# Sums of weight blocks in a two-layer hybrid trunk: two of four formed by accumulating transfers

## The chip, the cores and the metric

The kernel runs on one core of a Trainium2 chip. A core has TensorE for matrix products (PE in the profile, with its weight loader PEld), VectorE (DVE), ScalarE (ACT), GpSimd (POOL) and SyncE (SP), each with an instruction queue of its own that it works off in order, and sixteen DMA engines that all queues share. Waits between queues are on semaphores. The metric is the device time of one execution in microseconds; three runs of the kernel before gave 1565.7 to 1568.12, median 1567.72.

## The reference

Two layers act on 256 tokens of width 1024, all in float32. Each is a half-step SwiGLU feed-forward (FFN), a mixer, and a second FFN; a norm closes the trunk:

```python
for l in range(DEPTH):                       # DEPTH = 2
    h = h + 0.5 * swiglu(rms_norm(h, ffn1_norm[l]), ffn1_w_in[l], ffn1_w_out[l])
    u = rms_norm(h, mix_norm[l])
    ...
    h = h + merged @ w_out[l]
    h = h + 0.5 * swiglu(rms_norm(h, ffn2_norm[l]), ffn2_w_in[l], ffn2_w_out[l])
return rms_norm(h, final_norm)
```

`swiglu(x, w_in, w_out)` is `(silu(gate) * up) @ w_out`, with `gate` and `up` the halves of `x @ w_in` and 2816 inner channels. The mixer (a Mamba-2 branch beside a gated DeltaNet branch) is not touched by the change. There are four FFNs in all.

## The kernel before

**Forms.** All weights stand in one array `wst`, laid out in the order of use, in blocks of 128 x 1024 floats (512 KB). A block is loaded by SP into a raw slot (`wraw`, five slots, `NRAW`), then split for TensorE into a high half on ScalarE (`whi`, line 163) and a rest on VectorE (`wlo`, line 170). The profile names the lines of the helpers: 67 for `act` on ScalarE, 70 for `tt` and 73 for `stt` on VectorE. Such a pair is a form; there are five form slots (`NSPL`). Every product is three matmuls: high by high, low by high, high by low. A raw slot is free again when its block has been split, a form slot when the last product with it is done. `plan_ffn` writes the sequence of loads (`stream`) and of forms (`plan`) ahead of time; `take` gives the next form and keeps loads and splits running ahead by as many as the slots allow. The order of instructions on each engine's queue is set when the kernel is built, by a scheduler that goes by the order of writing and by when it reckons slots to be free; so a load into a slot that is free early can stand far ahead of its use.

**One FFN** follows the string `FFN`, `f` + 8 `c` + `A` + 4 `c` + `A` + 4 `c` + `A` + 2 `c` + `A` + 2 `c` + `BdBBBddddd`. `f` is a first chunk of 256 channels by tokens (four forms); each `c` is a chunk of 128 gate and 128 up channels (two forms, tile `fc`). The product with `w_out` is in part done by Winograd's form of Strassen's method, which needs seven products of 2 x 2 blocks in place of eight. Its weight blocks are b11, b12, b22 and b21, for two pairs of row blocks at a time, so a group has seven forms `q0` to `q6`, four in `A` (tiles `p`) and three in `B` (tiles `o`). Four groups cover sixteen row blocks; six blocks are multiplied directly (`d`). The closing stage is `BdBBBddddd`; in its last five `d` all five forms are needed within the first 15 matmuls, since the first half of the tokens goes through all five `d` before the second.

**Sums of blocks, before.** `A` loads b11 into a slot of its own (`wfirst`, tags `y0` to `y3`, four slots that the mixer uses too), and b12 and b22 into raw slots. Between its four splits VectorE does three subtractions in place (function `less`): `wfirst<-wraw,wfirst` twice and `wraw<-wraw` once. `B` loads b22 and b21 anew, subtracts once more, `wfirst<-wraw,wfirst`, and splits three forms. That is four subtractions a group, 64 in the kernel. The input's block sums, formed on VectorE by `block_sums` from a chunk's result `g2` (tiles `sf`), carry the matching signs. `join` adds the products of a pair's banks to `h` (eight VectorE instructions in two parts, on `h`, `u2`, `u4`, `u5`).

**GpSimd** does little here: it fills tiles with zeros in the mixer and computes powers (`rsqrt`, line 190), among them `zz`, the one that each norm waits for between `zz` on VectorE (line 78) and `hn`. The norm that follows an FFN runs while TensorE is at the second half of the last five `d`.

Of the kernel before, what the change touches and what calls it, by code (L numbers as in the profile page):

```python
# [52 lines left out]
def trunk_kernel(ctx, tc, x, wst, wsm, norms, lpar, rpar, cst, out):  # L53
# [32 lines left out]
    def trb(name):  # L86
        return trp.tile([P, 512], F32, tag="tr", name=name)
# [12 lines left out]
    def plan_plain(j, n):  # L100
        for i in range(j, j + n):
            stream.append(i)
            plan.append(("d", [len(stream) - 1], len(stream)))
        return j + n

    def plan_ffn(j):


        o, j2, held = j + 4 * FC, j + 4 * FC + 22, []
        for kind in FFN:  # L110
            if kind in "fc":
                j = plan_plain(j, 4 if kind == "f" else 2)
            elif kind == "d":
                o = plan_plain(o, 1)
            else:
                if kind == "A":
                    where = [len(stream) + i for i in range(3)]
                    stream.extend(range(o, o + 3))
                    held.append((where, o + 2))
                    o += 4  # L120
                    for i, need in enumerate((2, 3, 3, 3)):
                        plan.append((f"q{i}", where, where[0] + need))
                else:
                    where, b22 = held.pop(0)
                    where += [len(stream) + 1, len(stream)]
                    stream.extend([b22, b22 + 1])
                    for i in range(4, 7):
                        plan.append((f"q{i}", where, len(stream)))
        return j2
# [5 lines left out]
    n_raw = len(stream)  # L135
    first = {js[0] for kind, js, _ in plan if kind == "q0"}
    n_forms = len(plan)
    state = {"loaded": 0, "prepped": 0, "taken": 0, "last": None, "hold": False, "behind": {}, "first": 0}
    raws, halves = {}, {}

    def load(j):
# [5 lines left out]
        state["last"] = nc.sync.dma_start(r[:], wst[stream[j] // 2, :, (stream[j] % 2) * 1024 :][:, 0:1024])  # L147
        raws[j] = r

    def prep(i):  # L150
        kind, js, _ = plan[i]
        hi = wpool.tile([P, 1024], F32R, tag="whi", name="whi", bufs=NSPL)
        lo = wpool.tile([P, 1024], F32R, tag="wlo", name="wlo", bufs=NSPL)

        def less(o, a, b):
            tt(raws[js[o]][:], raws[js[a]][:], raws[js[b]][:], ALU.subtract)


        r = raws[js[{"q2": 1, "q4": 4, "q5": 3}.get(kind, 0)]]
        with ExitStack() as behind:  # L160
            for ins in state["behind"].pop(i, ()):
                behind.enter_context(tc.issue_after(ins))
            act(hi[:], r[:])
            if kind == "q1":
                less(1, 2, 1)
            elif kind == "q2":
                less(0, 2, 0)
            elif kind == "q4":
                less(0, 3, 0)
            tt(lo[:], r[:], f(hi[:]), ALU.subtract)  # L170
            if kind == "q0":
                less(0, 1, 0)
        for o in {"d": (0,), "q2": (1,), "q3": (2,), "q4": (4,), "q5": (3,), "q6": (0,)}.get(kind, ()):
            raws.pop(js[o])
        halves[i] = (hi, lo)
# [6 lines left out]
    def take():  # L182
        j = state["taken"]
        state["taken"] = j + 1
        ahead("loaded", min(plan[min(j + NSPL, n_forms) - 1][2] + NRAW - 1, n_raw), load)
        ahead("prepped", min(j + 1 if state["hold"] else j + NSPL, n_forms), prep)
        return halves.pop(j)
# [205 lines left out]
    def join(pb):  # L393
# [10 lines left out]
        stt(u5[:], pb[5][:], 0.5, u2[:], ALU.mult, ALU.add)  # L404
        tt(hv[1][0], hv[1][0], u2[:], ALU.add)
        tt(hv[1][1], hv[1][1], u5[:], ALU.add)
        yield
# [26 lines left out]
    def ffn(nxt):  # L434
# [19 lines left out]
        def block_sums(p, g2):  # L454
# [35 lines left out]
        for c in range(FC - 1):  # L490
# [18 lines left out]
            if todo[0] == "A":  # L509
                if not pb:  # L510
                    pb.update({i: trb(f"p{i}") for i in (1, 6, 5, 7)})
                four = [
                    (pb[1], lambda p: stat(2 * p, 0), PAIRS[n]),
                    (pb[5], lambda p: sums(p, 0), PAIRS[n]),
                    (pb[7], lambda p: sums(p, 2), PAIRS[n]),
# [849 lines left out]
```

## Time and profile before

| | |
|---|---|
| median of three runs | 1567.72 us |
| the profiled execution | 1568.61 us, span 1566.8 us |
| TensorE busy, granted clock | 98% of the span, 0.999 |
| VectorE busy | 80% |
| ScalarE busy | 61% |
| GpSimd busy | 3%, 60 instructions |
| transfers | 293.14 MB, 187 GB/s in the mean |

The profiled execution's own time is 1.8 us above its span and 0.9 us above the median. The busy shares are means over stages: TensorE's 98% says that little of the time is lost, and the view of waits says where. In a row of the order of time stand start, duration, engine, line, operation, result and operands, and in brackets the engine's idle time before it and what ended that. The loader (PEld) runs ahead of the products, so an idle time there is not lost in full.

### The profile page before, as it was taken

How to read it: one execution, taken by the hardware profiler on the slowest of the kernel's cores; microseconds unless marked ns; L12 is line 12 of the kernel's file. 1: busy time of each engine (PE TensorE's matmuls, PEld its weight loads, DVE VectorE, ACT ScalarE, POOL GpSimd, SP SyncE). 2: the span in 40 equal slices, each digit the busy share in tenths (PEclk: the TensorE clock that was granted, in tenths of full speed). 3: DMA queues.
4: the chain of work that ended last, by engine and by line, in shares of the span. 5: the costliest groups of instructions: out<-in, count | busy, mean ns of one | idle time of the engine just before them, and what ended most of it. 6: DMA issues, size and time to landing. Idle time of an engine off the chain costs nothing.

```text
span 1566.8 us, 28951 instructions
## 1 busy us (share of the span) xinstructions
PE 1535.5 (98%) x11452; PEld 1382.9 (88%) x11452; DVE 1252.7 (80%) x1888; ACT 949.7 (61%) x1534; POOL 53.7 (3%) x60
## 2 busy tenths in 40 slices
PE   8999999999999999999999999999999999999997
PEld 7999779999988888999799997899898888889995
DVE  6878869967899766878878887799589997677886
ACT  5656567766665545656555565676756665455554
POOL 0000010000000000000000002010000000000000
PEclk9999999999999999999999999999999999999999
DMA  8665565653565656565665557566445556556554
GB/s 294 215 203 178 197 215 175 179 160 113 177 215 162 193 198 196 170 212 188 229 215 189 174 186 223 182 190 188 116 136 202 175 178 209 192 179 192 170 185 134
DMA packets 94222, 293.14 MB, mean 187 GB/s; under 512 B 22325, under 2 KB 23301, under 8 KB 93062
## 3 DMA queue, kind: packets, MB, share of 16 engines
q1 hardware_dynamic: 94086, 291.29, 57.5%
q8 instruction: 90, 1.47, 0.4%
q14 instruction: 46, 0.38, 0.1%
HBM read 289.33 MB, written 1.92 MB: 186 GB/s over the span
## 4 chain that ended last, share of the span: by engine, by line
PE 67%; DVE 16%; DMA 6%; issue 5%; ACT 4%; POOL 1%; SPq 1%; POOLq 0%; ACTq 0%; DVEq 0%
PE fc L301 7%; PE fc L307 7%; DVE wlo L70 7%; PE fc L306 7%; DMA wraw<-in_wst_dram 5%; PE t L297 3%; PE t L296 3%; PE t L298 3%; PE b L298 3%; PE b L297 2%; PE b L296 2%; ACT whi L67 2%; DVE ca L73 1%; PE xs L301 1%; PE xs L306 1%
## 5 line engine op out<-in xcount | busy, mean ns | idle before, releaser
L70 DVE TENSOR_TENSOR wlo<-wraw,whi 128x1024 fp32r<-128x1024 f32 x488 | 591.3, 1220 | 173.2 <-ACT whi L67 165.2
L67 ACT ACTIVATE whi<-wraw 128x1024 fp32r<-128x1024 f32 x488 | 511.5, 1059 | 275.7 <-PE fc L306 85.5
L307 PE MATMUL fc<-uW,wlo 128*128 128x256 f32 x1280 | 354.7, 277 | 0.0
L301 PE MATMUL fc<-uW,whi 128*128 128x256 f32 x1280 | 354.0, 277 | 0.0
L306 PE MATMUL fc<-uW,whi 128*128 128x256 f32 x1260 | 348.1, 276 | 0.0
L301 PEld LDWEIGHTS fc<-uW,whi 128*128 128x128 f32 x1280 | 240.4, 188 | 0.8
L307 PEld LDWEIGHTS fc<-uW,wlo 128*128 128x128 f32 x1280 | 240.4, 188 | 0.0
L306 PEld LDWEIGHTS fc<-uW,whi 128*128 128x128 f32 x1260 | 236.5, 188 | 0.8
L67 ACT ACTIVATE whi<-wfirst 128x1024 fp32r<-128x1024 f32 x64 | 68.0, 1062 | 59.2 <-PE fc L306 34.0
L296 PE MATMUL t<-whi,uW 128*128 128x512 f32 x256 | 102.1, 400 | 0.0
L297 PE MATMUL t<-wlo,uW 128*128 128x512 f32 x256 | 100.8, 394 | 0.5 <-DVE wlo L70 0.5
L298 PE MATMUL t<-whi,uW 128*128 128x512 f32 x256 | 100.7, 394 | 0.0
L70 DVE TENSOR_TENSOR wlo<-wfirst,whi 128x1024 fp32r<-128x1024 f32 x64 | 78.0, 1218 | 6.8 <-ACT whi L67 5.9
L296 PE MATMUL b<-whi,bh 128*128 128x512 f32 x192 | 76.3, 399 | 0.0
L297 PE MATMUL o<-wlo,gh 128*128 128x512 f32 x160 | 65.4, 409 | 9.8 <-DVE wlo L70 9.6
L297 PE MATMUL b<-wlo,bh 128*128 128x512 f32 x192 | 74.9, 390 | 0.0
L298 PE MATMUL b<-whi,bl 128*128 128x512 f32 x192 | 74.3, 394 | 0.6 <-DVE bl L70 0.6
L70 DVE TENSOR_TENSOR wfirst<-wraw,wfirst 128x1024 f32<-128x1024 f32 x48 | 58.5, 1220 | 20.2 <-DMA wraw<-in_wst_dram 19.9
L301 PE MATMUL xs<-uW,whi 128*128 128x256 f32 x256 | 73.0, 285 | 0.0
L307 PE MATMUL xs<-uW,wlo 128*128 128x256 f32 x256 | 71.5, 279 | 0.0
L306 PE MATMUL xs<-uW,whi 128*128 128x256 f32 x256 | 71.3, 279 | 0.0
L298 PE MATMUL o<-whi,gl 128*128 128x512 f32 x160 | 62.6, 391 | 0.0
(319 smaller groups left out, 3401.3 us busy)
## 6 DMA issues: line engine op xcount, KB each, us to landing
wraw<-in_wst_dram SPq DMA_DIRECT2D x504, 512.0 KB, 4.7
wfirst<-in_wst_dram SPq DMA_DIRECT2D x16, 512.0 KB, 5.4
dc<-rdram SPq DMA_DIRECT2D x8, 1024.0 KB, 8.4
nw<-in_norms_dram SPq DMA_DIRECT2D x6, 512.0 KB, 6.1
gb<-rdram SPq DMA_DIRECT2D x8, 256.0 KB, 5.5
h<-in_x_dram SPq DMA_DIRECT2D x4, 256.0 KB, 5.5
out_dram<-fo SPq DMA_DIRECT2D x4, 256.0 KB, 2.0
dq<-X SPq DMA_DIRECT2D x2, 256.0 KB, 5.7
```

The costliest lines, as they stand in the source:

```text
L67: return A.activation(out=o, in_=i, func=func, **kw)
L70: return V.tensor_tensor(out=o, in0=a, in1=b, op=op)
L73: return V.scalar_tensor_tensor(out=o, in0=a, scalar=s, in1=b, op0=op0, op1=op1)
L296: PE.matmul(ps, lh, rh, start=start, stop=False)
L297: PE.matmul(ps, lh, rl, start=False, stop=False)
L298: return PE.matmul(ps, ll, rh, start=False, stop=stop)
L301: PE.matmul(ps, wh, mh, start=start, stop=False)
L306: PE.matmul(ps, wh, ml, start=False, stop=False)
L307: PE.matmul(ps, wl, mh, start=False, stop=stop)
```

## The change

A group now has one sum tile, `wsum`, in the slots that were `wfirst`'s. SP loads b11 into it, and GpSimd issues a transfer of b12 that adds to what is there (`accum_op`), so b11 + b12 is there without VectorE. `A` loads b12, b22 and, a second time, b11 into raw slots. VectorE adds b22 to the raw b12 and to `wsum`; after the last split of `A` (`q3`) GpSimd issues a second accumulating transfer, of b21, and the sum of all four blocks stands ready for `q6`. `B` loads b22 and b21 into raw slots, which are split as they are (`q4`, `q5`). So VectorE does two additions a group in place of four subtractions, SP loads six blocks a group in place of five (one into the sum tile), and GpSimd issues two accumulating transfers a group, 32 in all. Signs that the sums lose are moved to `block_sums` and `join`; the first two products of `A` change places. The loads ahead are now bounded by counting raw slots alone (`limit`).

```diff
     def plan_ffn(j):
...
+        for at, kind in enumerate(FFN):
+            if at in spots:
+                y = len(stream)
+                stream.extend([("y", o1 + 4 * q), ("+", o1 + 4 * q + 1, y)])
+                begun.append(y)
+                q += 1
...
+            elif kind == "A":
+                y, u = begun.pop(0), len(stream)
+                stream.extend([("w", o + 1), ("w", o + 2), ("w", o)])
+                plan.append(("q1", (y, u, u + 1), u + 2))
+                plan.append(("q0", (u + 2, y, u + 1), u + 3))
+                plan.append(("q2", (u,), u + 3))
+                plan.append(("q3", (y, o + 3), u + 3))
+                held.append((y, o + 2))
+                o += 4
...
+                y, b22 = held.pop(0)
+                stream.append(("w", b22))
+                plan.append(("q4", (len(stream) - 1,), len(stream)))
+                stream.append(("w", b22 + 1))
+                plan.append(("q5", (len(stream) - 1,), len(stream)))
+                plan.append(("q6", (y,), len(stream)))
...
+    def add_to(r, i):
+        G.dma_start(out=r[:], in_=tile_of(i), accum_op=ALU.add)
+
     def load(j):
-        if j in first:
-            r = slots.tile([P, 1024], F32, tag=f"y{state['first']}", name="wfirst")
+        kind, i = stream[j][:2]
+        if kind == "+":
+            add_to(raws[stream[j][2]], i)
+            return
+        if kind == "y":
+            r = slots.tile([P, 1024], F32, tag=f"y{state['first']}", name="wsum")
...
             act(hi[:], r[:])
-            if kind == "q1":
-                less(1, 2, 1)
-            elif kind == "q2":
-                less(0, 2, 0)
-            elif kind == "q4":
-                less(0, 3, 0)
+            if kind in ("q0", "q1"):
+                to, by = (raws[k][:] for k in js[1:])
+                tt(to, to, by, ALU.add)
             tt(lo[:], r[:], f(hi[:]), ALU.subtract)
-            if kind == "q0":
-                less(0, 1, 0)
...
+        if kind == "q3":
+            add_to(r, js[1])
...
-        stt(u4[:], pb[5][:], 0.5, u2[:], ALU.mult, ALU.add)
-        tt(hv[0][1], hv[0][1], u4[:], ALU.add)
+        stt(u4[:], pb[5][:], -0.5, u2[:], ALU.mult, ALU.add)
+        tt(hv[0][1], hv[0][1], u4[:], ALU.subtract)
...
-            tt(s1, a21, a22, ALU.add)
+            tt(s1, a21, a22, ALU.subtract)
             tt(s3, a11, a21, ALU.subtract)
             tt(s2_, s1, a11, ALU.subtract)
-            tt(s4, a12, s2_, ALU.subtract)
+            tt(s4, a12, s2_, ALU.add)
```

VectorE's queue in the first FFN, from the splits of the last chunk's blocks to the first forms of the second `B`. Before (`wfirst_567` and `wfirst_900` are the b11 slots of the first two groups, `wraw_1703` and `wraw_1741` their b21):

```order
L70 TENSOR_TENSOR wlo_1730<-wraw_1569,whi_1729 128x1024 [waits DMAHW7_49,Activation_49]
L70 TENSOR_TENSOR wfirst_567<-wraw_1703,wfirst_567 128x1024 [waits DMAHW1_49]
L70 TENSOR_TENSOR wlo_1746<-wraw_1691,whi_1745 128x1024 [waits DMAHW0_49,Activation_49]
L70 TENSOR_TENSOR wfirst_900<-wraw_1741,wfirst_900 128x1024 [waits DMAHW4_49]
L70 TENSOR_TENSOR wlo_1751<-wraw_1703,whi_1750 128x1024 [waits PE_49,Activation_49]
L70 TENSOR_TENSOR wlo_1808<-wfirst_567,whi_1807 128x1024 [waits PE_49,Activation_49]
L70 TENSOR_TENSOR g2_1739<-sg_1803,fc_1740 128x256 [waits Activation_49]
L73 SCALAR_TENSOR_TENSOR h_78<-p1_846,h_78 128x512 [waits Activation_49]
L73 SCALAR_TENSOR_TENSOR u2_1966<-p6_847,half_1965 128x512
L73 SCALAR_TENSOR_TENSOR u4_1967<-p5_848,u2_1966 128x512 [waits DVE_49]
L70 TENSOR_TENSOR wfirst_1230<-wraw_1811,wfirst_1230 128x1024 [waits DMAHW6_49]
L70 TENSOR_TENSOR wlo_1814<-wraw_1715,whi_1813 128x1024 [waits DMAHW2_49,PE_49,Activation_49]
```

The same place now (`wraw_1703` and `wraw_1715` are b22 and b21 of the first group, `wsum_358` its sum tile, `wraw_1727` the single `d`):

```order
L70 TENSOR_TENSOR wlo_1742<-wraw_1581,whi_1741 128x1024 [waits DMAHW3_49,Activation_49]
L70 TENSOR_TENSOR wlo_1756<-wraw_1703,whi_1755 128x1024 [waits DMAHW4_49,Activation_49]
L70 TENSOR_TENSOR wlo_1762<-wraw_1715,whi_1761 128x1024 [waits DMAHW5_49,PE_49,Activation_49]
L70 TENSOR_TENSOR wlo_1819<-wsum_358,whi_1818 128x1024 [waits DMASW4_49,PE_49,Activation_49]
L70 TENSOR_TENSOR g2_1751<-sg_1814,fc_1752 128x256 [waits Activation_49]
L73 SCALAR_TENSOR_TENSOR h_78<-p1_854,h_78 128x512 [waits Activation_49]
L73 SCALAR_TENSOR_TENSOR u2_1972<-p6_853,half_1971 128x512
L73 SCALAR_TENSOR_TENSOR u4_1973<-p5_852,u2_1972 128x512 [waits DVE_49]
L70 TENSOR_TENSOR h_78<-h_78,u4_1973 128x512 [waits DVE_49]
L70 TENSOR_TENSOR wlo_1825<-wraw_1727,whi_1824 128x1024 [waits DMAHW6_49,PE_49,Activation_49]
L73 SCALAR_TENSOR_TENSOR u2_1972<-p7_855,u2_1972 128x512
L70 TENSOR_TENSOR g2_1751<-sg_1876,fc_1817 128x256 [waits Activation_49]
```

The three subtractions are gone, two more joins stand ahead of the last chunk's `g2`, and the split of the sum tile waits on a semaphore of the accumulating transfers (DMASW).

GpSimd's queue between the mixer of the first layer and the third FFN, before (`zz_6769` and `zz_6805` are the powers of the norm into the second FFN, one for each half of the tokens, the last two those of the norm into the third):

```order
L190 TENSOR_TENSOR srr_6215<-sss_6207,mhalf_96 128x2 [waits DVE_49]
L190 TENSOR_TENSOR zz_6769<-zz_6769,mhalf_96 128x1 [waits DVE_49]
L190 TENSOR_TENSOR zz_6805<-zz_6805,mhalf_96 128x1 [waits DVE_49]
L190 TENSOR_TENSOR zz_8776<-zz_8776,mhalf_96 128x1 [waits DVE_49,Pool_49]
L190 TENSOR_TENSOR zz_8812<-zz_8812,mhalf_96 128x1 [waits DVE_49,Pool_49]
```

And now, from the second FFN's norm to the third's (`wsum_7015` to `wsum_7963` are the second FFN's sum tiles, `wsum_9030` to `wsum_9978` the third's):

```order
L212 TENSOR_TENSOR zz_6813<-zz_6813,mhalf_96 128x1 [waits DVE_49]
L165 DMA wsum_7015<-in_wst_dram 128x1024 [waits DVE_49]
L165 DMA wsum_7378<-in_wst_dram 128x1024 [waits DVE_49]
L165 DMA wsum_7715<-in_wst_dram 128x1024 [waits DVE_49]
L165 DMA wsum_7963<-in_wst_dram 128x1024 [waits DVE_49]
L165 DMA wsum_9030<-in_wst_dram 128x1024 [waits DMASW4_49,DMAHW5_49,DMASW0_49,DVE_49]
L165 DMA wsum_9393<-in_wst_dram 128x1024 [waits DMASW5_49,DMAHW1_49,DMASW1_49,DVE_49]
L165 DMA wsum_9730<-in_wst_dram 128x1024 [waits DMASW6_49,DMAHW4_49,DMASW2_49,DVE_49]
L165 DMA wsum_9978<-in_wst_dram 128x1024 [waits DMASW7_49,DMAHW4_49,DMASW3_49,DVE_49]
L212 TENSOR_TENSOR zz_8792<-zz_8792,mhalf_96 128x1 [waits DVE_49,Pool_49]
```

An FFN's four first accumulations stand together ahead of its four second ones (the second FFN's are the first four rows of transfers here), and the third FFN's first ones stand ahead of its own norm's powers.

SP's queue at the end of the second FFN, before (`wfirst_9886` and `wfirst_10166` are b11 slots of the third FFN):

```order
L147 DMA wfirst_9886<-in_wst_dram 128x1024 [waits DVE_49]
L147 DMA wraw_8601<-in_wst_dram 128x1024 [waits DMAHW6_49,DMAHW5_49,DVE_49]
L147 DMA wraw_8643<-in_wst_dram 128x1024 [waits DMAHW7_49,DVE_49]
L147 DMA wfirst_10166<-in_wst_dram 128x1024 [waits DVE_49]
L147 DMA wraw_8655<-in_wst_dram 128x1024 [waits DMAHW0_49,DVE_49]
```

Now (`wraw_8637` and `wraw_8659` are the last two `d`, the next four the third FFN's `f`, `wraw_8713` its first channel block):

```order
L177 DMA wsum_9730<-in_wst_dram 128x1024 [waits DMASW6_49,DVE_49]
L177 DMA wraw_8637<-in_wst_dram 128x1024 [waits DMAHW6_49,DMAHW5_49,DVE_49]
L177 DMA wraw_8659<-in_wst_dram 128x1024 [waits DMAHW7_49,DVE_49]
L177 DMA wraw_8671<-in_wst_dram 128x1024 [waits DMAHW0_49,DVE_49]
L177 DMA wraw_8683<-in_wst_dram 128x1024 [waits DMAHW2_49,DVE_49]
L177 DMA wraw_8695<-in_wst_dram 128x1024 [waits DMAHW3_49,DMAHW1_49,DVE_49]
L177 DMA wraw_8711<-in_wst_dram 128x1024 [waits DMAHW5_49,DVE_49]
L177 DMA wraw_8713<-in_wst_dram 128x1024 [waits DMAHW6_49,DVE_49]
L177 DMA wsum_9978<-in_wst_dram 128x1024 [waits DMAHW4_49,DMASW7_49]
```

The load for the third FFN's fourth sum tile has moved behind the last `d`, the four `f` and a channel block.

More of the change, by code (lines that the diff above doesn't have):

```diff
@@ L106, in plan_ffn @@
     def plan_ffn(j):
-        o, j2, held = j + 4 * FC, j + 4 * FC + 22, []
-        for kind in FFN:
+        o, j2, begun, held = j + 4 * FC, j + 4 * FC + 22, [], []
+        spots, q = [], 0
+        for at, kind in enumerate(FFN):
+            if kind == "A":
+                spots.append(at - 2)
+        o1 = o + FFN[: FFN.index("A")].count("d")
+        for at, kind in enumerate(FFN):
+            if at in spots:
[3 more added lines that the diff above has]
+                q += 1
             if kind in "fc":
@@ L135, in trunk_kernel @@
     n_raw = len(stream)
-    first = {js[0] for kind, js, _ in plan if kind == "q0"}
+    limit = []
+    for _, _, need in plan:
+        m, room = need, NRAW
+        while m < n_raw:
+            room -= stream[m][0] == "w"
+            if not room:
+                break
+            m += 1
+        limit.append(m)
     n_forms = len(plan)
@@ L184, in take @@
         state["taken"] = j + 1
-        ahead("loaded", min(plan[min(j + NSPL, n_forms) - 1][2] + NRAW - 1, n_raw), load)
+        ahead("loaded", limit[min(j + NSPL, n_forms) - 1], load)
         ahead("prepped", min(j + 1 if state["hold"] else j + NSPL, n_forms), prep)
@@ L510, in ffn @@
                 if not pb:
[L511 removed]
+                    pb.update({i: trb(f"p{i}") for i in (5, 6, 1, 7)})
                 four = [
+                    (pb[5], lambda p: sums(p, 0), PAIRS[n]),
                     (pb[1], lambda p: stat(2 * p, 0), PAIRS[n]),
[L514 removed]
                     (pb[7], lambda p: sums(p, 2), PAIRS[n]),
```

31 lines of the change are left out of this document (9 added, 22 removed).

## The prediction

> **What bounds the kernel now.** I read the busy times first, then who waits for whom on TensorE, then the order of time around the waits, then the transfers.
>
> ```profile
> PE 1535.5 (98%) x11452; PEld 1382.9 (88%) x11452; DVE 1252.7 (80%) x1888; ACT 949.7 (61%) x1534; POOL 53.7 (3%) x60
> ...
> PE o L297 <- DVE wlo L70: 9.6, 16, 1.4
> PE hnT L262 <- DVE hn L73: 5.1, 6, 0.9
> ...
> PEld o L297 <- DVE wlo L70: 21.6, 32, 1.8
> PEld hnT L262 <- DVE hn L73: 6.3, 4, 2.4
> ```
>
> TensorE is the bound: 98%. What another engine can give back is TensorE's waiting, and the last lines say where most of that is: 32 weight loads of the output products (`o`) waited 21.6 us for VectorE's low half `wlo` (total, times, longest). These are eight in each of the four closing stages of an FFN (the string `BdBBBddddd`); the stages with the products `p` have no such row. In order of time, in the first FFN (start, duration, then in brackets the idle time and its releaser):
>
> ```profile
> 140.34 0.39 PE L296 MATMUL p<-whi,gh 128*128 128x512 f32 x1
> 145.80 0.28 PE L301 MATMUL fc<-uW,whi 128*128 128x256 f32 x1
> 156.83 0.39 PE L296 MATMUL o<-whi,bsc 128*128 128x512 f32 x1
> 169.19 0.39 PE L296 MATMUL o<-whi,gh 128*128 128x512 f32 x1
> 170.05 0.39 PE L298 MATMUL o<-whi,gl 128*128 128x512 f32 x1
> 193.74 0.39 PE L296 MATMUL t<-whi,uW 128*128 128x512 f32 x1
> ...
> 169.71 0.19 PEld L297 LDWEIGHTS o<-wlo,gh 128*128 128x128 f32 x1 [0.56 <-DVE wlo L70]
> 179.45 0.19 PEld L297 LDWEIGHTS o<-wlo,gh 128*128 128x128 f32 x1 [1.21 <-DVE wlo L70]
> ```
>
> A group `A` is 24 matmuls from 140.34 to 145.80: 0.2275 us each. Two such steps should take 0.455; from 169.19 to 170.05 they took 0.86, so the 0.56 of idle loader cost 0.405, 0.16 less than it reads (the loader has slack). Over all: 21.6 - 32 x 0.16 = 16.5 us. This is the most that the change can win, if it touches nothing else.
>
> Why VectorE is late there:
>
> ```profile
> 147.32 1.22 DVE L70 TENSOR_TENSOR wfirst<-wraw,wfirst 128x1024 f32<-128x1024 f32 x1
> 148.45 1.22 DVE L70 TENSOR_TENSOR wlo<-wraw,whi 128x1024 fp32r<-128x1024 f32 x1
> 152.87 1.23 DVE L70 TENSOR_TENSOR wfirst<-wraw,wfirst 128x1024 f32<-128x1024 f32 x1 [3.19 <-DMA wraw<-in_wst_dram]
> 154.01 1.22 DVE L70 TENSOR_TENSOR wlo<-wraw,whi 128x1024 fp32r<-128x1024 f32 x1
> ...
> 158.70 1.23 DVE L70 TENSOR_TENSOR wfirst<-wraw,wfirst 128x1024 f32<-128x1024 f32 x1
> 167.30 1.23 DVE L70 TENSOR_TENSOR wfirst<-wraw,wfirst 128x1024 f32<-128x1024 f32 x1 [0.77 <-DMA wraw<-in_wst_dram]
> 178.19 2.34 DVE L70 TENSOR_TENSOR wlo<-wraw,whi 128x1024 fp32r<-128x1024 f32 x2
> 180.46 1.28 DVE L70 TENSOR_TENSOR h<-h,u 128x512 f32<-128x512 f32 x2
> 181.66 1.21 DVE L70 TENSOR_TENSOR wlo<-wraw,whi 128x1024 fp32r<-128x1024 f32 x1
> ...
> L70 DVE TENSOR_TENSOR g<-sg,fc 128x256 f32<-128x256 f32 x80 | 33.0, 413 | 0.0
> L70 DVE TENSOR_TENSOR gl<-g,gh 128x512 fp32r<-128x512 f32 x40 | 27.3, 683 | 0.0
> ```
>
> Four subtractions of the closing stage stand between the splits, and twice VectorE, whose queue is in order, idled at one whose block had not landed while splits of older blocks stood behind it (3.19 us at 152.87). Issue to issue a split costs 1.14 us (two from 178.19 to 180.46).
>
> Set T = 156.83, the first closing product. TensorE needs 18 x 0.2275 = 4.1 us for a `B`, 2.7 for the single `d`; the last five `d` start at T + 19.1 and take a new form every 3 x 0.2275 = 0.68, the fifth's low half at T + 22.05. Before, three of the eighteen forms were ready at T (five slots, two still with the last chunk). So VectorE owed 15 x 1.14 = 17.1, two subtractions 2.3, the eight joins of `h` and `u` 5.1 (two in 1.28 at 180.46), two `g` and a `gl` 1.5, and idled 0.77: 26.8 us for 22.05. It came 4.7 late; by the waits of this FFN and of the second, each in a window of its own, TensorE's loader stood 4.4 there:
>
> ```profile
> PEld o L297 <- DVE wlo L70: 4.4, 8, 1.2
> ...
> PEld o L297 <- DVE wlo L70: 6.6, 8, 1.8
> ```
>
> **The change, part by part.**
>
> ```profile
> L70 DVE TENSOR_TENSOR wfirst<-wraw,wfirst 128x1024 f32<-128x1024 f32 x48 | 58.5, 1220 | 20.2 <-DMA wraw<-in_wst_dram 19.9
> L70 DVE TENSOR_TENSOR wraw<-wraw 128x1024 f32<-128x1024 f32 x16 | 19.5, 1218 | 0.1
> L67 ACT ACTIVATE whi<-wfirst 128x1024 fp32r<-128x1024 f32 x64 | 68.0, 1062 | 59.2 <-PE fc L306 34.0
> ```
>
> *Subtractions removed.* 48 + 16 become 2 x 16 additions: 32 x 1.22 = 39 us off VectorE, 9.8 an FFN, two in each `A` and one in each `B`. In the `A` stages this buys nothing: TensorE does not wait there. In the closing stage all four go, and with them the queueing behind unlanded blocks. The order now has the joins ahead of T, save one `u5` and two `h`. Four forms are ready at T, so VectorE owes 14 x 1.14 + 1.1 (one `g`, one `gl`) + 1.9 (three joins) = 19.0 us for 22.05. The limit is then the five form slots: the fifth `d` gets its slot when the last `B` product ends, T + 19.1; 1.06 us on ScalarE (the `whi` row), 1.22 on VectorE and about 0.2 between give T + 21.6, 0.45 early. So the 16.5 us go, if the blocks land in time.
>
> *Loads added.* An FFN's plain loads grow from 70 to 74, and eight accumulating transfers come on top.
>
> ```profile
> q1 hardware_dynamic: 94086, 291.29, 57.5%
> ...
> wraw<-in_wst_dram SPq DMA_DIRECT2D x504, 512.0 KB, 4.7
> dc<-rdram SPq DMA_DIRECT2D x8, 1024.0 KB, 8.4
> ...
> 10.00:20.00 10.00, 9.22 (x35) 6.88 (x36) 8.82 (x12) 7.79 (x14) 0.56 (x1) 1.00 1.03 404
> ...
> 770.00:775.00 5.00, 3.83 (x14) 2.21 (x13) 4.87 (x6) 2.12 (x2) 0.00 (x0) 1.00 1.03 388
> ```
>
> 291.29 MB took 57.5% of 1566.8 us: 524,288 bytes cost 1.62 us of all sixteen engines, 1.30 at the best rate seen (404 GB/s). No accumulating transfer is in this trace. Its price P lies between a plain one's 1.3 and, since it fetches the block from HBM and the sum from SBUF, two plain ones' 3.24; I take 3.24, nearest to the row of the 1024 KB transfer, which lands in 8.4 us where 512 KB takes 4.7. Per FFN that is 74 x 1.62 + 8 x 3.24 = 146 us of the 183 between the first `f` (10.8) and 193.74: it fits. The tightest stretch is from the third `A` to the fourth, 5.46 + 11.03 = 16.5 us: seven plain loads and one accumulation, 11.3 + 3.2 = 14.6. With five raw slots and nine blocks in 19.1 us a block may take 10.6 us from issue to split; less the 2.3 of its two passes and some queueing, landing may take about 7.5. So no stall in three FFNs; I leave 0.5 us in each. The second FFN's closing stage also carries the third's four sums: nine blocks, three `y` loads and three accumulations in 22 us: 19.4 + 9.7 at the mean rate, 15.6 + 9.7 at the best. That is more than 22 and the limit that 770 to 775 already touched (share 1.03), but the sums are not due until the next FFN's first `A`, and blocks are up to five ahead; I take 2 us there, between 0 and the 6.6 - 8 x 0.16 = 5.3 that its waits cost now.
>
> The Trainium skill, "Collectives: The Full Stack", section "The bandwidth ceiling: the fold count and why AG ≠ RS ≠ AR", says that an adding transfer runs at half the rate of a copy, not for the addition but because it has two source reads. By it P would be 3.24, by the plain row 1.62, and the sum 1.5 us smaller; no run here shows it yet.
>
> *What joins GpSimd's queue.* 32 transfers. Ahead of the power of the norm between FFN 2 and 3 now stand the third FFN's four first accumulations, the last waiting for a `y` load that SP has behind the load for the first channel chunk, whose slot the fifth `d` frees.
>
> ```profile
> 780.56 0.55 POOL L190 TENSOR_TENSOR zz<-zz,mhalf 128x1 f32<-128x1 f32 x1 [174.24 <-DVE zz L78]
> ...
> DMA to landing us min/median/max: 3.4/5.4/7.9
> ```
>
> By the numbers above that load goes out at T + 21.7 and lands at T + 25.1 to 29.6 (the `wfirst` range); the power is due at about T + 28, 1.9 after the last product of the first half. Delay 0 to 1.6 us and the issue itself (0.2 to 2.2, GpSimd's own instructions); I take 1. The other norms' accumulations are issued long before. The number of forms, hence of splits on ScalarE and VectorE, stays; the signs and the order of two products change no count. Both cost nothing with no cover needed.
>
> Sum: 16.5 - 1.5 - 2 - 1 = 12 us off the profiled 1568.6, that is 1556.6; the median of the runs is 0.9 below the profiled one, so 1556.
>
> **Rivals.**
>
> *The accumulating transfers starve the raw blocks: slower.* Place: `A` to `A` and the closing stages. For it: at 5.1 us the 16.5-us stretch is full (11.3 + 5.1), and a block that lands 1 us later costs a fifth of that for each of some 14 blocks. Against it: traffic averages 57.5%, and P would have to be three plain transfers. From 5.1 it decides. At 7 the stretch overruns by 1.8 in each FFN and the closing stages keep their waits: 1568.6 + 7 = 1576; at 10 an FFN needs 120 + 80 = 200 us for 183, +68. I price it at 1580. Chance 0.25.
>
> *The waits change their name only.* The closing stage waits for landing blocks instead of subtractions: for it, the 3.19 us at 152.87 are a transfer's; against it, that block was the ninth ahead and held back splits whose data were there. Half to four fifths of the wait stays: 1562 to 1567. Chance 0.13.
>
> *GpSimd's queue.* The delayed power alone costs at most 3.8 us, once; it only widens the other two. If accumulations are issued late as well because GpSimd's issue crawls beside VectorE, it ends near 1572. Chance 0.04. Against it: fills of 1.81 us on GpSimd left a split beside them at 1.22:
>
> ```profile
> 973.72 1.81 POOL L660 MEMSET AT<- 128x2048 f32 x1
> ...
> 973.39 1.22 DVE L70 TENSOR_TENSOR wlo<-wraw,whi 128x1024 fp32r<-128x1024 f32 x1
> ```
>
> **Numbers.** Forecast 0.58 (own range 1549 to 1560: all 16.5 us and the lowest run's 2.9 below the profiled one at one end, only 8 us won at the other). The second rival is half a gain over 0.2% (3.1 us, about what a measurement of this kernel can tell from no change), half within it. Faster 0.58 + 0.06 = 0.64, same 0.07, slower 0.25 + 0.04 = 0.29. The range to 1582 takes in the slower cases up to P of about 7.
>
> **What would show it.** Right: the wait of `o` L297 for `wlo` falls from 21.6 to below 7, no new wait in `p` or `fc`; the VectorE groups of 48 and 16 become two of 16; a second queue of 16.8 MB appears and plain loads land in 5 to 6 us. Wrong: `fc` or `p` waits for whi or wlo with a transfer behind it, landing beyond 7.5 us, or GpSimd's `zz` starts some us after VectorE's.

## The result, and the profile after

The changed kernel takes 1559.73 us (median of six runs, 1556.05 to 1564.55), the kernel before beside it 1567.05 (six runs, 1565.7 to 1568.85): a ratio of 0.9951, 95% interval 0.9939 to 0.9963, so 7.3 us or 0.49% faster. The profiled execution took 1558.56 us with a span of 1556.8, which is 10.0 less than the span before. The forecast was 12 us less, 1556.

From the page of the changed kernel, the busy times, the transfer queues (packets, MB, share of the engines) and the landing times from issue:

```profile
PE 1530.0 (98%) x11452; PEld 1384.0 (89%) x11452; DVE 1216.8 (78%) x1856; ACT 946.5 (61%) x1534; POOL 82.6 (5%) x92
...
q1 hardware_dynamic: 96390, 299.68, 57.5%
q0 software_dynamic: 4608, 16.78, 6.2%
...
wraw<-in_wst_dram SPq DMA_DIRECT2D x520, 512.0 KB, 4.9
wsum<-in_wst_dram POOLq DMA_DIRECT2D x32, 512.0 KB, 8.0
wsum<-in_wst_dram SPq DMA_DIRECT2D x16, 512.0 KB, 6.4
```

From its view of waits, those of the loader (total, times, longest):

```profile
PEld hnT L284 <- DVE hn L73: 8.1, 5, 2.7
PEld o L319 <- DVE wlo L70: 3.9, 4, 1.1
...
PEld o L318 <- ACT whi L67: 2.6, 3, 2.2
```

And VectorE's groups of additions (busy, mean ns, idle time ahead):

```profile
L70 DVE TENSOR_TENSOR wraw<-wraw 128x1024 f32<-128x1024 f32 x16 | 19.6, 1225 | 37.1 <-DMA wraw<-in_wst_dram 37.1
L70 DVE TENSOR_TENSOR wsum<-wsum,wraw 128x1024 f32<-128x1024 f32 x16 | 19.5, 1219 | 0.1
```

The wait for the low half fell from 21.6 us in 32 waits to 3.9 in 4, the groups of 48 and 16 subtractions are two of 16 additions, and a second queue of 16.78 MB is there. New is a wait for `whi` of 2.6 us, and the wait for the norm (`hnT`) grew by 1.8. No row of `p` or `fc` is among the waits. VectorE waits 37.1 us for blocks at the first addition of `A`, but TensorE does not feel it.

Where the time went shows best in the four closing stages, each from its first product `o` to the first product of what follows (the fourth, which has nothing behind it, to its own last product). In windows cut at these starts (length, then busy time and count of TensorE, its loader, VectorE, ScalarE and GpSimd; granted clock, transfers' share, GB/s), first the kernel before:

```profile
156.80:193.70 36.90, 35.37 (x154) 27.27 (x153) 31.84 (x37) 22.04 (x26) 0.55 (x1) 1.00 0.58 194
747.10:786.20 39.10, 35.55 (x154) 27.25 (x153) 33.01 (x39) 22.03 (x26) 0.55 (x1) 1.00 0.69 237
931.00:968.00 37.00, 35.56 (x155) 27.31 (x154) 32.09 (x38) 22.05 (x26) 0.55 (x1) 1.00 0.60 196
1522.10:1559.80 37.70, 34.44 (x146) 26.20 (x144) 30.51 (x37) 18.44 (x23) 0.55 (x1) 1.00 0.43 139
```

And the changed kernel:

```profile
156.60:190.10 33.50, 33.50 (x155) 27.82 (x153) 27.76 (x32) 22.18 (x26) 0.56 (x1) 1.00 0.61 202
743.10:784.30 41.20, 36.02 (x154) 28.64 (x153) 26.94 (x30) 21.96 (x26) 4.03 (x5) 0.96 0.83 255
928.80:963.50 34.70, 33.94 (x154) 27.81 (x153) 28.43 (x33) 22.06 (x26) 0.56 (x1) 1.00 0.58 198
1516.60:1549.60 33.00, 32.76 (x145) 26.81 (x145) 26.08 (x30) 18.57 (x23) 0.56 (x1) 1.00 0.44 144
```

By the exact starts three stages are 2.2 to 4.7 us shorter, and the second is 2.1 longer. In sum that is 8.2 us; the other 1.8 of the profiled gain are small shifts elsewhere, 1.4 of it in the two mixers. The second stage is the one with GpSimd's four transfers in it (4.03 us of GpSimd, 5 instructions) and with a granted clock of 0.96.

What happens there in the changed kernel, in the order of time (start, duration, then in brackets the idle time and its releaser):

```profile
766.74 1.06 ACT L67 ACTIVATE whi<-wraw 128x1024 fp32r<-128x1024 f32 x1 [2.68 <-DMA wraw<-in_wst_dram]
767.85 0.50 PE L318 MATMUL o<-whi,gh 128*128 128x512 f32 x1 [1.74 <-ACT whi L67]
769.70 0.63 PE L320 MATMUL o<-whi,gl 128*128 128x512 f32 x1
770.12 0.63 PE L318 MATMUL o<-whi,gh 128*128 128x512 f32 x1
...
776.15 0.21 DVE L78 TENSOR_SCALAR zz<-ss 128x1 f32<-128x1 f32 x1 [0.79 <-ACT junk L67]
778.34 0.86 POOL L165 DMA_DIRECT2D wsum<-in_wst_dram  x1 [15.27 <-DMA wsum<-in_wst_dram]
778.90 0.88 POOL L212 TENSOR_TENSOR zz<-zz,mhalf 128x1 f32<-128x1 f32 x1
780.62 0.66 PE L284 MATMUL hnT<-cs,hn 128*128 128x128 f32 x4 [1.92 <-DVE hn L73]
```

Two windows there, with the columns of the windows above:

```profile
765.40:768.80 3.40, 1.21 (x3) 0.45 (x3) 0.98 (x1) 1.06 (x1) 0.00 (x0) 0.99 1.06 298
769.00:772.50 3.50, 3.40 (x9) 2.73 (x10) 0.74 (x2) 0.72 (x2) 0.00 (x0) 0.55 1.02 359
```

And its transfers from 743 to 775 us, the queue of the accumulations and the median landing times:

```profile
q0 software_dynamic: 432, 1.57, 25.7%
...
wraw<-in_wst_dram SPq DMA_DIRECT2D x12, 512.0 KB, 7.6
wsum<-in_wst_dram POOLq DMA_DIRECT2D x3, 512.0 KB, 9.2
```

Three things add up. The blocks land in 7.6 us here, for a median of 4.9 over the whole kernel, while the transfers' share is at 1.02 to 1.06: ScalarE waits 2.68 us for one, and TensorE behind it. Then the clock is granted at half speed for about 3.4 us: a matmul every 0.42 in place of 0.2275, some 1.7 us lost. And GpSimd issues the third FFN's fourth accumulation, whose tile's first load landed only then, ahead of the norm's power: VectorE's `zz` is done at 776.36, the power starts at 778.90, and TensorE stands 1.92.

### The profile page after: what moved, and what is told of

The parts are those of the page before. It is cut to its first block, busy times and chain, and to the rows that moved or that the text cites. A ratio compares the mean times of both kernels' runs of the same rounds, so it can differ in the third digit from the quotient of the medians.

```text
span 1556.8 us, 28984 instructions
## 1 busy us (share of the span) xinstructions
PE 1530.0 (98%) x11452; PEld 1384.0 (89%) x11452; DVE 1216.8 (78%) x1856; ACT 946.5 (61%) x1534; POOL 82.6 (5%) x92
## 3 DMA queue, kind: packets, MB, share of 16 engines
q1 hardware_dynamic: 96390, 299.68, 57.5%
q0 software_dynamic: 4608, 16.78, 6.2%
HBM read 314.50 MB, written 1.92 MB: 203 GB/s over the span
## 4 chain that ended last, share of the span: by engine, by line
PE 78%; DVE 10%; DMA 5%; ACT 3%; issue 3%; POOL 1%; SPq 0%; POOLq 0%; ACTq 0%; DVEq 0%
PE fc L329 9%; PE fc L323 9%; PE fc L328 9%; DVE wlo L70 5%; PE t L319 3%; PE t L320 3%; PE t L318 3%; PE b L320 3%; DMA wraw<-in_wst_dram 3%; PE b L319 3%; PE b L318 2%; PE o L320 2%; PE p L319 2%; PE o L319 2%; PE p L320 2%
## 5 line engine op out<-in xcount | busy, mean ns | idle before, releaser
L70 DVE TENSOR_TENSOR wlo<-wraw,whi 128x1024 fp32r<-128x1024 f32 x504 | 610.7, 1220 | 167.6 <-ACT whi L67 161.1
L67 ACT ACTIVATE whi<-wraw 128x1024 fp32r<-128x1024 f32 x504 | 527.5, 1058 | 273.9 <-PE fc L328 83.9
L67 ACT ACTIVATE whi<-wsum 128x1024 fp32r<-128x1024 f32 x48 | 50.8, 1059 | 30.1 <-PE fc L328 25.2
L70 DVE TENSOR_TENSOR wlo<-wsum,whi 128x1024 fp32r<-128x1024 f32 x48 | 58.6, 1220 | 12.8 <-ACT whi L67 12.7
L318 PE MATMUL o<-whi,gh 128*128 128x512 f32 x160 | 63.2, 395 | 1.7 <-ACT whi L67 1.7
```

Source lines behind the costliest of these rows:

```text
L67: return A.activation(out=o, in_=i, func=func, **kw)
L70: return V.tensor_tensor(out=o, in0=a, in1=b, op=op)
L318: PE.matmul(ps, lh, rh, start=start, stop=False)
```

## The experiments

The runs lay on several chips, on which the kernel before took 1567.1 to 1570.4 us, so each is compared with the kernel before on its own chip. The lengths of the four closing stages, in us, are from each kernel's profiled execution.

| kernel | ratio to before, 95% interval | FFN 1 | FFN 2 | FFN 3 | FFN 4 |
|---|---|---|---|---|---|
| before | 1 | 36.9 | 39.1 | 36.9 | 37.7 |
| changed | 0.9951 (0.9939 to 0.9963) | 33.6 | 41.2 | 34.7 | 33.0 |
| changed, again | 0.9952 (0.9939 to 0.9964) | 35.9 | 41.9 | 34.3 | 33.2 |
| no_closing_less | 0.9897 (0.9880 to 0.9915) | 33.6 | 33.6 | 33.6 | 32.4 |
| no_less | 0.9895 (0.9878 to 0.9913) | 33.7 | 33.8 | 33.6 | 32.4 |
| no_plus | 0.9890 (0.9874 to 0.9905) | 33.6 | 33.6 | 33.6 | 33.0 |
| fourth_behind | 0.9955 (0.9943 to 0.9968) | 37.0 | 39.1 | 36.6 | 32.4 |
| plus_behind | 0.9926 (0.9913 to 0.9938) | 36.8 | 34.2 | 34.4 | 33.1 |
| sums_in_order | 1.0019 (1.0009 to 1.0029) | 35.8 | 36.2 | 36.8 | 33.8 |
| plus_twice | 1.0117 (1.0098 to 1.0136) | 36.6 | 51.4 | 36.0 | 35.6 |
| pool_less | 0.9974 (0.9962 to 0.9985) | 36.1 | 36.6 | 36.0 | 36.8 |
| six_raw | 0.9917 (0.9905 to 0.9929) | 33.6 | 33.6 | 33.6 | 32.4 |
| late_add | 0.9935 (0.9920 to 0.9950) | 34.5 | 35.5 | 34.2 | 36.8 |
| six_raw_late_add | 0.9878 (0.9860 to 0.9896) | 33.6 | 33.5 | 33.6 | 32.4 |

The theory: the closing subtractions on VectorE are the loss and the change removes it; what it loses again is the transfers' crowding and GpSimd's queue at the end of the second FFN. The rivals: VectorE's load weighs everywhere; the accumulations cost everywhere; or they cost nothing and the plain loads do.

### What VectorE's subtractions cost

**no_closing_less**

```diff
-            elif kind == "q4":
-                less(0, 3, 0)
```

> The kernel before, with the one subtraction in each B left out (16 of 64; the products of these blocks are then wrong), nothing else changed. The closing stages of the kernel before are 16.9 us longer in sum than those of the kernel without accumulations. If VectorE's debt in the closing stages is the loss, four subtractions of 1.14 us less there, and no block to wait for in them, leave a debt of some 1 to 2 us a stage at most: 10 to 15 us less than the kernel before. If the blocks' landing sets it (the rival of waits that change their name), 5 us or less.

Measured: 1552.06 us for 1568.46, 16.4 less. All four stages have the length of TensorE's work alone, called bare from here on: 33.6 us, and 32.4 for the fourth. The window of the second:

```profile
744.10:777.70 33.60, 33.60 (x154) 27.90 (x154) 27.58 (x31) 22.07 (x26) 0.55 (x1) 1.00 0.77 254
```

TensorE is busy all of the window, and no wait of `o` for `wlo` is left among the waits. The gain is above the 10 to 15 expected: no debt of 1 to 2 us a stage stayed.

**no_less**

```diff
         def less(o, a, b):
-            tt(raws[js[o]][:], raws[js[a]][:], raws[js[b]][:], ALU.subtract)
+            pass
```

> The kernel before, with all 64 subtractions left out (its products are wrong), the loads as they were. First theory: the closing stages fall to 33.6 us each and nothing else moves, 16 to 18 us less than the kernel before and within 3 us of the kernel without the subtraction in B, since in the stages A TensorE does not wait for VectorE. Second: VectorE's 80% weighs on every stage, then the other 48 subtractions bring as much again and the chunks and groups A get shorter too, over 20 us less.

Measured: 1551.94, 16.5 less. The 48 subtractions of `A`, 58 us of VectorE, are worth 0.1 us, which is nothing that can be told apart. So the 16 in `B` are the whole loss, and the rival that VectorE weighs everywhere falls.

### What the accumulations cost

**again**: the changed kernel once more, unaltered.

> The changed kernel once more, for its spread and for a second profile. If the slow clock in the second FFN's closing stage (0.50 for 3.4 us from 768.85) is a regular part of the change, the same stage shows it again and the median lies at 1558 to 1561. If it is chance, the stage may go without it, and the profiled run is then some 1.6 us shorter for that alone.

Measured: 1561.9 for 1569.64. The second stage is as long again, 41.9 us, with 3.10 us of TensorE's wait for the norm; the slow clock came behind that wait and lay over the stage's last products. That some slow stretch comes is not chance: the mean granted clock is 0.996 to 0.998 in each of the eleven executions of the changed kernel, and 0.999 in eleven of the fifteen of the kernel before on this chip. What moves from one execution to the next is the first FFN's closing stage: 35.9 us here for 33.6, from the same instructions.

**no_plus**

```diff
     def add_to(r, i):
-        G.dma_start(out=r[:], in_=tile_of(i), accum_op=ALU.add)
+        pass
```

> All 32 accumulating transfers are left out (so the sums are not formed); everything else stays. First theory: what the accumulations cost lies in the second FFN's closing stage alone (4.5 us of loader waits there, 1.6 of slow clock, 2.1 for the norm's power behind the fourth accumulation): 5 to 7 us less, 1553 to 1555 by median, and the other three FFNs keep their lengths within 0.5 us. Second theory: the accumulations slow the blocks everywhere: all four FFNs get shorter, 1549 or less. Third: the accumulations are hidden and the plain loads do it: within 2 us of the changed kernel, the waits for whi stay at 768 and 769.

Measured: 1552.34, that is 17.3 less than before and 9.6 less than the changed kernel beside it. The closing stages are the bare 33.6 us, and the clock does not fall. The cost is more than the first theory's 5 to 7 us. Between the two profiled executions (spans of 1562.3 and 1550.3) 8.3 us lie in the second FFN's closing stage, but 2.3 in the first's and 0.9 in the others. By the starts of their products, chunks and groups `A` are the same to 0.1 us with and without accumulations. So the accumulations cost in closing stages alone, and 74 plain loads an FFN in place of 70 cost nothing that can be seen. How they reach the first of these stages is open: none is issued in it, and the last one ahead of it (at 144.80 in "again") is 12.7 us earlier. What can be seen is a late block: ScalarE waited 4.12 us for one until 153.61 there, 3.8 ahead of the stage, and in the first profile 3.83 until 150.67, 5.9 ahead.

### Queue or transfers

**fourth_behind**

```diff
-            add_to(raws[stream[j][2]], i)
+            with ExitStack() as behind:
+                if state["first"] == 0:
+                    behind.enter_context(tc.issue_after(state["pow"].ins))
+                add_to(raws[stream[j][2]], i)
```

> Only the fourth of the first accumulations of an FFN is queued on GpSimd behind the power of that FFN's norm; the other three, and all plain loads, stay where they are. If the queue and the transfers are two costs that add, this takes back the 2.1 us of the power alone: 1.5 to 2.5 us less than the changed kernel, and the second FFN's closing stage keeps its loader waits of some 4.5 us and the slow clock. If the wait for the power was hidden behind the late blocks, or the fourth accumulation also slows the blocks, 0 or over 4.

Measured: 1561.79 for 1568.46, the changed kernel's ratio. In its profiled execution TensorE waits no more for the norm at that place; in the order of time VectorE's part and GpSimd's power start 0.36 us apart:

```profile
783.46 0.21 DVE L78 TENSOR_SCALAR zz<-ss 128x1 f32<-128x1 f32 x1 [0.79 <-ACT junk L67]
...
783.82 0.56 POOL L215 TENSOR_TENSOR zz<-zz,mhalf 128x1 f32<-128x1 f32 x1 [13.41 <-DVE zz L78]
```

The second stage is 39.1 us, 2.1 shorter than the changed kernel's, and keeps its late blocks and slow clock, as expected. But stages 1 and 3 were longer in this execution, which was among the slowest of its twelve (1557.77 to 1566.86); the median shows no gain. The queue's 2 us are seen in place, and not in the whole.

**plus_behind**

```diff
-            add_to(raws[stream[j][2]], i)
+            with tc.issue_after(state["pow"].ins):
+                add_to(raws[stream[j][2]], i)
```

> Only the four first accumulations of an FFN are queued on GpSimd behind the power of that FFN's norm; the loads of the tiles stay where they are. First theory: the power starts 0.4 us after VectorE's part again (2.1 us back) and the second FFN's closing stage has three accumulations less, some 9 us of all sixteen engines, so the waits of 4.5 us and the slow clock go too: 1553 to 1556. If the three plain loads of the sums are enough to fill the stage, only the 2.1 come back: 1557 to 1558.

Measured: 1557.48, 4.4 less than the changed kernel beside it. The second closing stage falls from 41.9 to 34.2 us, although the plain loads of the sums are still issued in it (at 754.3, 758.9 and 770.7 us). So it was the accumulations that filled it, and with them the slow clock is gone from the stage. The range of its runs is 3 us for 5 (five runs each); the first stage is 36.8 in the profiled one.

**sums_in_order**

```diff
+SPOTS = [4, 8, 12, 16]
...
-        spots, q = [], 0
-        for at, kind in enumerate(FFN):
-            if kind == "A":
-                spots.append(at - 2)
+        spots, q = SPOTS, 0
...
+                behind.enter_context(tc.issue_after(state["last"].ins))
```

> The plain load of each sum is queued on SP behind the block load that stands before it in the stream, at chunks 4, 8, 12 and 16 of its own FFN, so neither these loads nor the accumulations can run in the closing stage of the FFN before. First theory: 1552 to 1555, the second FFN's closing stage is as short as the first's (waits under 1 us, no slow clock, no wait for the norm at the third FFN's start), the rest unchanged. Rival: the transfers only move, and chunks or groups A of the same FFN now wait (fc or p waits for whi): 1558 or more.

Measured: 1572.62, slower than before; the rival holds. In its view of waits are such of `fc` and `p` that the changed kernel has not:

```profile
PEld o L319 <- DVE wlo L71: 11.6, 21, 1.1
...
PEld p L319 <- DVE wlo L71: 3.9, 7, 1.0
PEld fc L329 <- DVE wlo L71: 3.7, 5, 1.1
```

By the starts of its stages, four chunks took up to 23.5 us for 21.9 and an `A` up to 6.4 for 5.46, some 8 us in FFN 2 to 4. In the changed kernel the scheduler has put the first loads of FFN 2 and 4, and so their first accumulations, into the mixers (from 526.7 and 1300.3 us), where nothing waits for them. Where they run decides what they cost.

### How far from the threshold

**plus_twice**

```diff
-        G.dma_start(out=r[:], in_=tile_of(i), accum_op=ALU.add)
+        for _ in range(2):
+            G.dma_start(out=r[:], in_=tile_of(i), accum_op=ALU.add)
```

> Every accumulating transfer is issued twice (the sums are then wrong), so one sum takes 6.0 us of all sixteen engines for 3.0 and the kernel moves 33.6 MB on this queue. By the prediction's threshold (5.1 us) the stretch from the third A to the fourth overruns by about 1 us in each FFN and the closing stages keep waits: slower than the kernel before, 1572 or more by median. Rival: the accumulations hurt only where they stand in the second FFN's closing stage and in GpSimd's queue: 5 to 8 us over the changed kernel, all of it at the end of the second FFN.

From its page, the queue of the accumulations, and a window of the second closing stage:

```profile
q0 software_dynamic: 9216, 33.56, 11.7%
...
780.00:785.00 5.00, 2.81 (x4) 1.08 (x4) 2.37 (x2) 2.00 (x2) 1.75 (x2) 0.50 1.03 357
```

Measured: 1587.56, 19.1 more than before. At 2.9 us each (11.7% of the 1586.5 us span over 64 transfers), a sum step takes 5.8 us of all engines, above the 5.1 at which the prediction had it decide, and slower it is. The place is mostly another: 17.8 us over 33.6 lie in the second closing stage, where TensorE did four matmuls in 5 us at half clock (the clock was at half for 13.7 us of this stage, which can cost 6.8 at most); the three others are 2.4 to 3.2 over, and chunks and groups of the first FFN 4.3.

### A better version

The first runs say that 16 subtractions are the loss, so they could go to GpSimd, with no transfer added.

**pool_less**

```diff
             elif kind == "q4":
-                less(0, 3, 0)
+                G.tensor_tensor(out=raws[js[0]][:], in0=raws[js[3]][:], in1=raws[js[0]][:], op=ALU.subtract)
```

> The kernel before with its 16 closing subtractions on GpSimd in place of VectorE, no accumulating transfer, the 48 others left on VectorE. [...] If a subtraction takes GpSimd over some 5 us, or slows VectorE's splits beside it, the last form of a B waits for it: 0.995 to 1.01.

Measured: 1564.78 for 1569.37, 4.6 less where 16 were to be had. GpSimd's group of them:

```profile
L169 POOL TENSOR_TENSOR wfirst<-wraw,wfirst 128x1024 f32<-128x1024 f32 x16 | 44.1, 2758 | 563.3 <-DMA wraw<-in_wst_dram 419.5 <-DVE wlo L70 143.8
```

And in the order of time, GpSimd and VectorE in the first FFN's closing stage:

```profile
156.93 3.05 POOL L169 TENSOR_TENSOR wfirst<-wraw,wfirst 128x1024 f32<-128x1024 f32 x1 [1.07 <-DMA wraw<-in_wst_dram]
...
158.56 2.51 DVE L70 TENSOR_TENSOR wlo<-wraw,whi 128x1024 fp32r<-128x1024 f32 x1
...
164.74 2.62 POOL L169 TENSOR_TENSOR wfirst<-wraw,wfirst 128x1024 f32<-128x1024 f32 x1 [4.75 <-DMA wraw<-in_wst_dram]
...
165.60 2.30 DVE L70 TENSOR_TENSOR h<-h,u 128x512 f32<-128x512 f32 x1
```

A subtraction takes GpSimd 2.76 us, but VectorE's split beside it took 2.51 for 1.22 and its `h` 2.30 for 0.69: 1.3 and 1.6 us lost, about what the subtraction had cost on VectorE. In sum VectorE is busy 1254.3 us, for 1236.5 in no_closing_less with the same 1872 instructions: 17.8 more, or 1.1 for each of the 16. Up to 1.7 us of the fourth stage's 36.8 are a slow clock in this one execution.

The other way, **six_raw**: keep the accumulations behind the norm and give the blocks a sixth raw slot. (The scratch tiles that make room are 128 x 512, 2 KB a partition.)

```diff
-NRAW = 5
+NRAW = 6
...
-    s2 = ctx.enter_context(tc.tile_pool(name="s2", bufs=9))
+    s2 = ctx.enter_context(tc.tile_pool(name="s2", bufs=7))
```

> The kernel with the first accumulations behind the norm, and six raw slots in place of five, with seven in place of nine of the half-kilobyte-wide scratch tiles to make room. If what the accumulations still cost in the closing stages (3.2, 0.6, 0.9 and 0.1 us over 33.6 in its profile) is blocks that land late for want of slots, the sixth slot takes it away: 0.989 to 0.991 of before. If it is the transfers' rate, or if seven scratch tiles make VectorE and ScalarE wait, 0.993 or more.

Measured: 1556.41 for 1569.37, 13.0 less. All closing stages are bare, so what the accumulations had still cost there was a want of slots (the step from nine to seven scratch tiles was not tried alone). But the stretch from the third `A` to the fourth has grown by 0.7 to 1.9 us in each FFN, 5.4 in all, and in the order of time VectorE waits there at an addition:

```profile
128.06 1.23 DVE L70 TENSOR_TENSOR wraw<-wraw 128x1024 f32<-128x1024 f32 x1 [2.86 <-DMA wraw<-in_wst_dram]
```

`g` and the chunk's splits stand behind it. The additions were then moved one form later, each behind that form's split, with six slots (**six_raw_late_add**) and, as a control, with five (**late_add**). In `plan_ffn` the tiles to add go with `q0` and `q2` accordingly.

```diff
-            if kind in ("q0", "q1"):
-                to, by = (raws[k][:] for k in js[1:])
-                tt(to, to, by, ALU.add)
-            tt(lo[:], r[:], f(hi[:]), ALU.subtract)
+            done = tt(lo[:], r[:], f(hi[:]), ALU.subtract)
+        if kind in ("q0", "q2"):
+            to, by = (raws[k][:] for k in js[1:])
+            with tc.issue_after(done.ins):
+                tt(to, to, by, ALU.add)
```

> The kernel with six raw slots, and in each A the two additions one form later, queued on VectorE behind the split of the form ahead of which they stood. In the profile of six_raw all closing stages are 33.6 us or less, and what is lost to the kernel without accumulations lies in the stretch from the third A to the fourth (12.9, 12.2, 12.7, 11.7 for 11.03 us), where VectorE stood 2.86 us at such an addition for a block that had not landed. If that queueing is the loss, the stretch falls to 11.03 and the kernel to 0.988 to 0.990 of before; if the blocks are late for all, it stays at 0.991 or more.

> The same later additions with five raw slots and nine scratch tiles (the kernel with the first accumulations behind the norm, otherwise). Its stages A lost nothing before, so no gain there; the closing stages still have blocks that land late: 0.991 to 0.993 of before, as without the edit. If the block's slot held one form longer delays the next load, slower: 0.994 or more.

Measured with six: 1550.28 for 1570.4, 20.1 less, a ratio of 0.9878 (0.9860 to 0.9896). It is faster than both kernels. How much of that is the sixth slot's own is open, as the kernel before was not run with six: from the closing stages to the next FFNs' first products the two mixers take 815.1 us here and 817.8 in the kernel before, one execution each, and accumulations left out do not shorten them (817.9 in no_plus). VectorE idles no more at the additions, by its group:

```profile
L70 DVE TENSOR_TENSOR wraw<-wraw 128x1024 f32<-128x1024 f32 x16 | 19.5, 1218 | 0.0
```

With five: 1559.76, 0.9935 (0.9920 to 0.9950), hardly different from 0.9926 without the edit. The fourth `A` takes 5.8 to 5.9 us for 5.46 there in every FFN, and the last stage is 36.8, up to 1.7 of it a slow clock in this execution. The later addition holds a raw slot longer, and pays only with the sixth.

## Why the prediction was right, and where not

**The bound of 16.5 us: right.** Without the closing subtractions 16.4 us go, without any 16.5.

**Subtractions in `A` buy nothing: right,** 0.1 us. **VectorE has time enough in the closing stage: right.** Where no accumulation crowds it, the stage is TensorE's bare work, and the five form slots with the last `d` cost nothing.

**The price P, taken as 3.24 us: 3.0.** 6.2% of 1556.8 us over 32 transfers is 3.0; a plain block is now 1.57 (299.68 MB in 57.5%). The ratio is 1.9. The Trainium skill's half rate for adding transfers ("Collectives: The Full Stack", section "The bandwidth ceiling: the fold count and why AG ≠ RS ≠ AR") agrees, though it is told there of collectives. Plain loads land in 4.9 us over the whole kernel, just under the 5 to 6 named.

**0.5 us in each of three FFNs: right for this execution, by luck** (0, 1.1 and 0.5 over the bare stages, 1.7 for 1.5). The first stage alone was 2.3, 3.2 and 3.5 over in three other executions (again, plus_behind, fourth_behind). The limit I gave on landing, 7.5, left no margin in a stage with five raw slots; with a sixth slot the excess was gone.

**2 us in the second FFN's closing stage: this step failed in size.** The stage is 7.6 over its bare 33.6; 2.1 of that are GpSimd's queue, and 5.5 stay. I counted 25 us of transfers against 22 and then let the sums give way: "the sums are not due until the next FFN's first `A`, and blocks are up to five ahead". None gave way: the blocks shared the engines with the sums and landed in 7.6 us. Right behind the late blocks the clock fell to half, some 1.7 us that no term had. With both, the stage passed the upper end that I gave, 5.3.

**GpSimd's queue, taken as 1 us: 2.1.** The mechanism is as told: the fourth accumulation, held by its tile's load, ahead of the power. T, the stage's first product, is 743.10 there. SP issued that load at T + 26.7, not T + 21.7, but the stage itself was 5 us late, and VectorE's part of the norm was done as much later, at T + 33.3 for T + 28. What failed is the landing: GpSimd could go on 8.5 us after the load's issue, for the 3.4 to 7.9 that I had from the kernel before, so the power came 2.5 us behind VectorE's part. I had added two costs as if independent, and the crowding of the first made the second larger.

**The sum: 10.0 in the profiles for 12,** and 7.3 in the medians. In the profiles the closing stages give 17.5 us back against their bare lengths, and lose 1.7 in three of them and 7.6 in the second: 9.3 for the 4.5 that I had put there, and 8.2 in sum. The 1.8 from elsewhere that make it 10.0 were in no term: that is luck. So is part of the median's place, 1559.73, just inside the range to 1560. The gain was forecast rightly, and the costs at half of what came. Between the profiles and the medians lies which execution was profiled: the one of before is 1.6 above its median, the one of after 1.2 below its own. Its runs spread over 8.5 us, those of before over 3.2; the working carried the old kernel's offset over.

**The rivals.** That the transfers starve the blocks is what happened in one stage of four, and it makes the kernel slower than before once the price is doubled or the sums run among the chunks. That waits only change their name is true of the same stage: `whi` behind a landing block in place of `wlo` behind a subtraction. GpSimd's queue stayed below its bound of 3.8.

## What to carry to other kernels

Ask of a busy engine not what its work is in sum but where its queue is late: 16 of 64 equal instructions held all of the 16 us, and the other 48 were free. Work that is moved to the transfers delays blocks that are due sooner (they landed in 7.6 us for 4.9), so place it by stage: the same 32 accumulations cost 9.6 us as the scheduler had put them, 5 when kept out of one closing stage, and made the kernel slower than before among the chunks. Then look at what the moved work now waits in front of: an addition that waits for a block holds up every split queued behind it.

## What the runs showed of the hardware

- An accumulating transfer of 512 KB costs 3.0 us of all sixteen engines, for 1.57 of a plain one, lands in 8.0 to 9.2 us, and takes GpSimd 0.88 us to issue.
- TensorE's clock fell to half for 3.4 us after stretches with waits in them: in the changed kernel TensorE was busy 1.21 of the 3.40 us ahead of it. The Trainium skill ("TensorE: Matmul & The Clock Gate", section "What's actually happening") tells of half rate after an idle window of about 3.4 us; the trace agrees in the length, but the window here was a third busy. Among the profiled executions it fell in the second closing stage of the changed kernel, again, fourth_behind and plus_twice, in the fourth one of pool_less and late_add, and in the second mixer of plus_behind and plus_twice; in the kernel before and the rest only after the last product. In plus_twice it stayed low for 10.24 and 6.83 us too, three and two times 3.41. In the 3.40 us ahead of the first drop TensorE was busy 1.67 us there, 1.72 in late_add and 2.09 in pool_less, so the stretch need not be idle. At what busy share the clock falls was not settled.
- GpSimd's two-input subtraction cost a VectorE instruction with two inputs beside it 1.3 to 1.6 us, where a fill beside a split cost nothing (1.22, quoted above). The Trainium skill ("SBUF — State Buffer", section "Who interferes with whom") has this rule: a VectorE instruction with two SBUF inputs contends with a GpSimd instruction that reads SBUF, not with one that only writes. The traces agree on both sides.
